# HGRN2 scan of a decoder step: sample outputs as rows on four groups of 32 TensorE columns, and scores of levels 32 and 64 on all column groups

## The chip, the cores and the metric

The kernel runs on one core of a Trainium2 chip. The metric is the device time of one execution in microseconds (us), as the median over the runs of a kernel.

## The reference

One inference step of a hybrid decoder layer: a SwiGLU half step, an input projection, an HGRN2 group of 4 heads (key and value size 128) beside a Mamba-2 group, an output projection, and a second SwiGLU half step. There are 1048 tokens: 16 meta tokens and 1024 prompt tokens, which are one sequence, and 8 samples of one token each, every one with a state of its own. Per HGRN2 head and sequence:

```
f = lb + (1-lb) sigmoid(u_f);  k = 1 - f;  v = u_i;  q = silu(u_q)
S_t = diag(f_t) S_{t-1} + k_t v_t^T          # 128x128
o_t = S_t^T q_t
```

For a sample that is one update of its state and one product of the updated state with its q. For the prompt the kernel computes the same by chunks of 128 tokens.

## The kernel before, in words

The phases follow one another: the first SwiGLU step, the input projection, the Mamba-2 scan, the four HGRN2 heads, the output projection, the second SwiGLU step. TensorE (PE) executes in the order in which the program is written. The order of the other engines (DVE, ACT, POOL, and SP, which issues the DMAs) is made by a scheduler, from dependencies and its own costs; an edit anywhere can so move instructions of theirs that it doesn't touch.

**Cover.** Between the steps of a head PE works off matmuls of the input projection that are still due, as `Fill` hands them out: `fill(n)` puts n steps of three matmuls (L163 to L165, some 350 columns each, 128x128 weights) into PE's order. While PE does these, DVE and ACT prepare the head's next step.

**One head** (`hgrn_scan`, L1713 to L1917). Its tensors lie with the 128 features on partitions and tokens along the free axis. First v is transposed; the columns of q, f and kg (k) that belong to the 8 samples are copied into a small tile qs, which has one buffer (L1740 to L1742). Then comes a tree of levels m = 1, 2, 4, ..., 64. A level computes scores within each chunk of 128 tokens, between the first and the second half of every block of 2m tokens, and then multiplies q of the second halves and k of the first by products of f (L1847 and L1848 on DVE). The next level's scores need these products, and L1847 and L1848 of a level need its scores to have been read. After each level stands a `fill` of 5 to 9 steps.

- Diagonal blocks (L1778) and levels below 32 (L1816): tiles of 32 stationary columns, round the four column groups of the array.
- Level 32 (L1807): for each of 8 chunks two matmuls of 32 stationary and 32 moving columns, which go to groups 0 and 2. ACT copies them into pp (L1810), two copies.
- Level 64: for each chunk one matmul of 64 stationary and 64 moving columns, always on the first 64 columns of the array; one copy.

**Samples of a head.** `load` (L1748) brings four states and, spread over the partitions, four rows v. `samples` (L1754) makes k v on ACT (L1758) and f S + k v on DVE (L1759). `outputs` (L1790) makes S^T q: it stands behind the scores of level 32 for samples 0 to 3 and behind those of level 64 for samples 4 to 7. For each sample the state, 128x128, is the stationary tile, and one column of q moves (L1792); the four results are columns of one PSUM tile, which ACT copies into os8 (L1793).

**After the tree.** kg is transposed in eight 128x128 pieces (L1873) and one of 16 columns (L1876), ACT copies these to kt and kt8 (L1874, L1877), `fill(4)`, state products of each chunk (L1887), a chain of DVE steps over the chunk states (L1892, L1895), `fill(6)`, and the chunks' outputs (L1906, L1908). os8 is first read after the scan, where the head's output is normalised (L1926, L1931).

**Mamba samples.** The updates of the 8 Mamba samples' states are independent of the heads: loads (L1538, L1539), a scaling on ACT (L1543), an update on DVE (L1544), a reduction on DVE (L1551), a store (L1552). The scheduler puts most of them into the time of head 0.

Tiles of 128x512 for state data come from a ring of 8 buffers (names r), 256-column tiles from a ring of 9 (names t), PSUM tiles for all of this from a ring of 4 (names mis).

Of the kernel before, what the change touches and what calls it, by code (L numbers as in the profile page):

```python
# [12 lines left out]
AF = mybir.ActivationFunctionType  # L13
ALU = mybir.AluOpType
# [3 lines left out]
P = 128  # L18
# [4 lines left out]
TP = NM + SEQ  # L23
NS = 8
T = TP + NS
# [1687 lines left out]
def hgrn_scan(K, a, o, hd, u, fill):  # L1713

    nc = K.nc
    q, f, kg, v = u["q"], u["f"], u["k"], u["v"]
# [3 lines left out]
    def small(tag, r, w=P):  # L1720
        return K.sml.tile([r, w], F32, tag=tag, name=K.uid(tag), bufs=1)
# [5 lines left out]
    for half in range(2):  # L1727
        ps = K.psm()
# [4 lines left out]
    ps = K.psm()  # L1733
# [3 lines left out]
    nc.scalar.copy(vs8, ps[:8, P : 2 * P])  # L1737
    vd = K.dram.tile([8, P], F32, name=K.uid("vd"))
    nc.sync.dma_start(vd, vs8)
    qs = small("qs", P, 24)  # L1740
    for i, src in enumerate((q, f, kg)):
        nc.scalar.copy(qs[:, 8 * i : 8 * i + 8], src[:, TP:T])  # L1742


    states = {}

    def load(b0):
        sb = K.raw().rearrange("p (b v) -> p b v", b=4)  # L1748
        vb = K.raw().rearrange("p (b v) -> p b v", b=4)
        nc.sync.dma_start(sb, a["state_hgrn"][0, b0 : b0 + 4, hd].rearrange("b k v -> k b v"))  # L1750
        nc.sync.dma_start(vb, vd[b0 : b0 + 4].partition_broadcast(P))
        states[b0] = sb, vb

    def samples(b0):  # L1754
        sb, vb = states[b0]
        for i in range(4):
            b = b0 + i
            nc.scalar.activation(vb[:, i], vb[:, i], AF.Identity, scale=qs[:, 16 + b : 17 + b])  # L1758
            nc.vector.scalar_tensor_tensor(sb[:, i], sb[:, i], qs[:, 8 + b : 9 + b], vb[:, i], ALU.mult, ALU.add)  # L1759
        nc.sync.dma_start(o["hgrn_sample"][0, b0 : b0 + 4, hd].rearrange("b k v -> k b v"), sb)  # L1760
        states[b0] = sb

# [7 lines left out]
    pv = pp.rearrange("p (c t) -> p c t", c=8)  # L1770
# [3 lines left out]
    ps = K.psm()  # L1774
# [11 lines left out]
    load(0)  # L1786
    os8 = small("os8", P, NS)

    def outputs(b0):
        ps = K.psm()  # L1790
        for i in range(4):
            nc.tensor.matmul(ps[:, i : i + 1], states[b0][:, i], qs[:, b0 + i : b0 + i + 1], start=True, stop=True)  # L1792
        nc.scalar.copy(os8[:, b0 : b0 + 4], ps[:, 0:4])  # L1793

    copies, copies8 = [diagonal], [small_diagonal]
    fe = f
    for li, m in enumerate(LEVELS):
        nb = 64 // m
        w = TP if m < 16 else 1024
        ps = K.psm()  # L1800
        qv = qf[:, :1024].rearrange("p (c b s i) -> p c b s i", c=8, s=2, i=m)
        if m >= 32:

            for c in range(8):
                for b in range(nb):
                    r = slice(2 * m * b, 2 * m * b + m)
                    nc.tensor.matmul(ps[r, m * c : m * c + m], kg[:, P * c + 2 * m * b : P * c + 2 * m * b + m], qv[:, c, b, 1], start=True, stop=True)  # L1807
            for b in range(nb):
                r = slice(2 * m * b, 2 * m * b + m)
                nc.scalar.copy(pv[r, :, 2 * m * b + m : 2 * m * b + 2 * m], ps[r, : 8 * m].rearrange("p (c i) -> p c i", c=8))  # L1810
        else:
            nb = 16 // m
            for c in range(8):
                for j in range(4):
                    r = slice(32 * j, 32 * j + 32)
                    nc.tensor.matmul(ps[r, 16 * c : 16 * c + 16], kg[:, P * c + 32 * j : P * c + 32 * j + 32], qv[:, c, nb * j : nb * j + nb, 1], start=True, stop=True)  # L1816

            def copy(m=m, nb=nb, ps=ps):
                pvm = pd.rearrange("p c (b s i) -> p c b s i", s=2, i=m)[:, :, :, 1]
                nc.vector.copy_predicated(pvm, K.mask[m].rearrange("p (b i) -> p b i", i=m)[:, None].broadcast_to([P, 8, nb, m]), ps[:, :P].rearrange("p (c b i) -> p c b i", c=8, i=m))  # L1820
                if m == 16:
                    for r in range(0, P, 32):
                        nc.scalar.copy(pv[r : r + 32, :, r : r + 32], pd[r : r + 32])

            copies.append(copy)
        if li == 0:
            s8 = K.psm()
            nc.tensor.matmul(s8[:16, 64:80], kg[:, 1024:TP], q[:, 1024:TP], start=True, stop=True)
        if m < 16:
            q8 = qf[:, 1024:TP].rearrange("p (b s i) -> p b s i", s=2, i=m)  # L1830
            nc.tensor.matmul(s8[:16, 8 * li : 8 * li + 8], kg[:, 1024:TP], q8[:, :, 1], start=True, stop=True)

            def copy8(li=li, m=m):
                nc.vector.copy_predicated(p8.rearrange("p (b s i) -> p b s i", s=2, i=m)[:, :, 1], K.mask[m][:16, 0:8].rearrange("p (b i) -> p b i", i=m), s8[:16, 8 * li : 8 * li + 8].rearrange("p (b i) -> p b i", i=m))

            copies8.append(copy8)
        if m >= 32:
            outputs({32: 0, 64: 4}[m])
        n = w // (2 * m)
        fv = fe[:, : w // m].rearrange("p (b s) -> p b s", s=2)  # L1840
        qw = qf[:, :w].rearrange("p (b s i) -> p b s i", s=2, i=m)
        kw = kg[:, :w].rearrange("p (b s i) -> p b s i", s=2, i=m)
        mid = 512 // (2 * m)
        with K.tc.high_priority(1000):
            for bs in (slice(0, mid), slice(mid, n)):
                k = bs.stop - bs.start
                nc.vector.tensor_mul(qw[:, bs, 1], qw[:, bs, 1], fv[:, bs, 0:1].broadcast_to([P, k, m]))  # L1847
                nc.vector.tensor_mul(kw[:, bs, 0], kw[:, bs, 0], fv[:, bs, 1:2].broadcast_to([P, k, m]))  # L1848
        fn = fp.tile([P, n])
        nc.vector.tensor_mul(fn, fv[:, :, 0], fv[:, :, 1])  # L1850
        if m == 8:
            f16 = fn
        fe = fn
        for copy in copies:
            copy()
        copies = []
        if m == 8:
            for copy in copies8:
                copy()
        if m == 4:  # L1860
            load(4)
        if m in (2, 16):
            samples({2: 0, 16: 4}[m])
        fill((9, 9, 8, 8, 7, 7, 7)[li] if hd < 3 else 7 if li < 2 else 5)
# [4 lines left out]
    for half in range(2):  # L1869
        ps = K.psm()  # L1870
# [4 lines left out]
    ps = K.psm()  # L1875
    nc.tensor.transpose(ps[:16, 0:P], kg[:, 1024:TP], K.ident)  # L1876
    nc.scalar.copy(kt8, ps[:16, 0:P])  # L1877
    fill(4)
    ss = K.slot("s", w=1024).rearrange("p (c v) -> p c v", c=8)
    s9 = small("s9", P, P)  # L1880
    for part in range(3):
        pu = K.psm()
        cc = range(4 * part, min(4 * part + 4, NC))
        for c in cc:
            i = c - 4 * part
            lk, lv = (kt[:, P * c : P * c + P], vt[:, P * c : P * c + P]) if c < 8 else (kt8, vt8)
            nc.tensor.matmul(pu[:, i * P : (i + 1) * P], lk, lv, start=True, stop=True)  # L1887
        for c in cc:
            i = c - 4 * part
# [11 lines left out]
    for half in range(2):  # L1901
        po = K.psm()
        for i in range(4):
            c = 4 * half + i
# [4 lines left out]
        c0 = NM if half == 0 else 0  # L1909
# [172 lines left out]
def body(ctx, tc, a, o):  # L2082
# [172 lines left out]
    with K.tc.manual_schedule(engines={mybir.EngineType.PE}):  # L2255
# [8 lines left out]
        for hd in range(NH):  # L2264
            fill.until(f"v{hd}")
            fill(4)
            if hd == 3:
                fill.jobs, fill.period = [lambda i=i: opa.update({i: split_opa(i)}) for i in (0, 2, 1, 3)], 13
            pieces = hgrn_scan(K, a, o, hd, us[hd], fill)
            g = us[hd]["g"] if hd < 3 else None  # L2270
            if hd == 0:
                fill.jobs, fill.period = jobs, 4
            if hd < 3:
                fill.until(f"g{hd}")
                hgrn_out(K, hd, pieces, g, "s", fill)
            if hd == 2:
                fill.until("z0")
                fill(10)
                ssm_norm(K, 0, "s", fill)
            if hd < 2:  # L2280
                spill(hd, g)
            elif hd == 2:
                kept.append(g)
# [160 lines left out]
```

## Time and profile before

| what | us |
|---|---|
| runs of before | 1937.75, 1937.73, 1942.81 |
| median | 1937.75 |
| span of the profiled execution | 1938.2 |
| PE busy in it | 1911.5 (99%) |
| DVE busy | 1533.1 (79%) |
| ACT busy | 845.8 (44%) |
| POOL busy | 96.8 (5%) |

The profile is of one further execution; the page gives its span and no other time for it. Its rows name engine, line, operation, the tile written and the tiles read, and sizes as partitions times elements; "x4" is a count of instructions. A bracket such as [1.57 <-DVE u L1848] is idle time of the engine just before the row, and what ended it. Ends of matmuls are modelled, so starts are what to subtract.

### The profile page before, as it was taken

How to read it: one execution, taken by the hardware profiler on the slowest of the kernel's cores; microseconds unless marked ns; L12 is line 12 of the kernel's file. 1: busy time of each engine (PE TensorE's matmuls, PEld its weight loads, DVE VectorE, ACT ScalarE, POOL GpSimd, SP SyncE). 2: the span in 40 equal slices, each digit the busy share in tenths (PEclk: the TensorE clock that was granted, in tenths of full speed). 3: DMA queues.
4: the chain of work that ended last, by engine and by line, in shares of the span. 5: the costliest groups of instructions: out<-in, count | busy, mean ns of one | idle time of the engine just before them, and what ended most of it. 6: DMA issues, size and time to landing. Idle time of an engine off the chain costs nothing.

```text
span 1938.2 us, 41058 instructions
## 1 busy us (share of the span) xinstructions
PE 1911.5 (99%) x16571; PEld 1882.1 (97%) x16571; DVE 1533.1 (79%) x2802; ACT 845.8 (44%) x1639; POOL 96.8 (5%) x155
## 2 busy tenths in 40 slices
PE   7999999999999999999999999999999999999998
PEld 7999999999999999999999989999999999999997
DVE  8888888888788777575766567998888888878965
ACT  8432322323534644475553455742232333354353
POOL 5000000000000410000000002200000000000000
PEclk9999999999999999999999999999999999999999
DMA  7232333325977542221544154233333333587862
GB/s 229 78 116 83 101 104 94 110 90 170 302 233 234 165 150 57 61 93 40 156 133 109 42 168 148 70 109 102 93 100 96 108 99 110 162 249 228 281 184 78
DMA packets 324071, 258.48 MB, mean 133 GB/s; under 512 B 17761, under 2 KB 299617, under 8 KB 323873
## 3 DMA queue, kind: packets, MB, share of 16 engines
q1 hardware_dynamic: 323640, 255.80, 43.5%
q8 instruction: 131, 2.15, 0.5%
q14 instruction: 60, 0.48, 0.1%
q0 software_dynamic: 224, 0.04, 0.0%
q10 hardware_dynamic: 16, 0.00, 0.0%
HBM read 191.84 MB, written 64.01 MB: 132 GB/s over the span
## 4 chain that ended last, share of the span: by engine, by line
PE 92%; DVE 4%; ACT 2%; issue 1%; DMA 1%; DVEq 0%; POOL 0%; ACTq 0%; POOLq 0%
PE acc L163 27%; PE acc L165 27%; PE acc L164 27%; PE mis L163 2%; PE mis L164 2%; PE mis L165 2%; PE mis L1816 1%; PE mis L1464 0%; PE mis L1887 0%; PE mis L1460 0%; ACT u L348 0%; PE mis L1792 0%; DVE t L303 0%; PE mis L1455 0%; PE mis L1906 0%
## 5 line engine op out<-in xcount | busy, mean ns | idle before, releaser
L163 PE MATMUL acc<-u,ws 128*128 128x258 f32 (+4 forms) x4226 | 1235.7, 293 | 0.7 <-DVE u L1095 0.3
L164 PE MATMUL acc<-u,ws 128*128 128x258 f32 (+4 forms) x4226 | 1225.2, 290 | 2.4 <-DVE u L354 2.2
L165 PE MATMUL acc<-u,ws 128*128 128x258 f32 (+4 forms) x4226 | 1225.7, 290 | 1.4 <-DVE ws L468 1.3
L164 PEld LDWEIGHTS acc<-u,ws 128*128 128x128 f32 x4226 | 802.1, 190 | 5.3 <-DVE u L354 2.8
L163 PEld LDWEIGHTS acc<-u,ws 128*128 128x128 f32 x4226 | 799.7, 189 | 4.2 <-issue 1.0
L165 PEld LDWEIGHTS acc<-u,ws 128*128 128x128 f32 x4226 | 798.9, 189 | 2.3 <-DVE ws L468 1.9
L468 DVE TENSOR_TENSOR ws<-r,ws 128x512 fp32r<-128x512 f32 x276 | 190.2, 690 | 73.5 <-ACT ws L464 73.3
L464 ACT CAST ws<-r 128x512 fp32r<-128x512 f32 x276 | 160.2, 616 | 15.3 <-ACT ws L464 8.6
L460 DVE TENSOR_TENSOR r<-r,r 128x512 f32<-128x512 f32 x176 | 121.5, 691 | 1.7 <-DMA r<-in_w_ffn_up_dram 0.2
L683 ACT ACTIVATE t<-t 128x516 f32<-128x516 f32 (+1 forms) x41 | 26.2, 639 | 211.1 <-DVE t L671 211.1
L714 ACT ACTIVATE t<-t 128x524 f32<-128x524 f32 (+1 forms) x47 | 30.0, 639 | 196.8 <-DVE t L671 196.8
L850 DVE TENSOR_TENSOR u<-u,u 128x1048 fp32r<-128x1048 f32 (+3 forms) x84 | 97.0, 1156 | 5.5 <-ACT u L846 5.1
L232 POOL TENSOR_TENSOR t<-t,t 128x262 f32<-128x262 f32 (+1 forms) x56 | 56.8, 1024 | 800.6 <-ACT t L231 690.9
L671 DVE TENSOR_TENSOR t<-t,u 128x524 f32<-128x524 f32 (+1 forms) x135 | 93.0, 696 | 2.9
L158 DVE TENSOR_TENSOR ws<-r,ws 128x512 fp32r<-128x512 f32 x88 | 60.8, 702 | 35.8 <-ACT ws L157 35.6
L907 ACT CAST ws<-u 128x512 fp32r<-128x512 f32 (+1 forms) x72 | 42.1, 585 | 102.6 <-DVE u L902 102.6
L846 ACT CAST u<-u 128x1048 fp32r<-128x1048 f32 (+3 forms) x84 | 82.8, 988 | 0.0
L907 ACT CAST ws<-r 128x512 fp32r<-128x512 f32 (+1 forms) x84 | 48.0, 582 | 70.9 <-DVE r L902 32.1
L936 DVE SCALAR_TENSOR_TENSOR s<-acc,s 128x524 f32<-128x524 f32 (+3 forms) x86 | 53.8, 648 | 31.5 <-PE acc L165 31.3
L912 DVE TENSOR_TENSOR ws<-r,ws 128x512 fp32r<-128x512 f32 (+1 forms) x84 | 56.3, 680 | 22.8 <-ACT ws L907 22.8
L157 ACT CAST ws<-r 128x512 fp32r<-128x512 f32 x88 | 54.0, 618 | 36.5 <-PE acc L165 31.0
L912 DVE TENSOR_TENSOR ws<-u,ws 128x512 fp32r<-128x512 f32 (+1 forms) x72 | 47.4, 658 | 26.5 <-ACT ws L907 26.5
(444 smaller groups left out, 2324.7 us busy)
## 6 DMA issues: line engine op xcount, KB each, us to landing
r<-in_w_ffn_down_dram SPq DMA_DIRECT2D x128, 256.0 KB
hd<-s SPq DMA_DIRECT2D x93, 258.0 KB
r<-in_w_ffn_gate_dram SPq DMA_DIRECT2D x88, 256.0 KB
r<-in_w_ffn_up_dram SPq DMA_DIRECT2D x88, 256.0 KB
hd<-s SPq DMA_DIRECT2D x77, 262.0 KB
u<-hd SPq DMA_DIRECT2D x36, 516.0 KB
u<-hd SPq DMA_DIRECT2D x28, 524.0 KB
r<-in_w_in_dram SPq DMA_DIRECT2D x56, 256.0 KB
```

What stands on the lines that cost most here:

```text
L158: self.nc.vector.tensor_sub(lo, src, hi.bitcast(F32))
L163: mm(ps, whi, xhi, start=first, stop=False, skip_group_check=more)
L164: mm(ps, whi, xlo, start=False, stop=False, skip_group_check=more)
L165: mm(ps, wlo, xhi, start=False, stop=last, skip_group_check=more)
L460: self.K.nc.vector.tensor_tensor(self.raw[p], self.raw[x], self.raw[y], op)
L464: self.K.nc.scalar.copy(self.w[p][:, : self.n * P], self.raw[p])
L468: self.K.nc.vector.tensor_sub(t[:, 512 : 512 + w], self.raw[p], t[:, :w].bitcast(F32))
L671: nc.vector.tensor_mul(t, t if src is None else src, spread.lanes(i, cs))
L846: K.nc.scalar.copy(hi, lo.bitcast(F32))
L850: K.nc.vector.tensor_sub(lo, lo.bitcast(F32), hi.bitcast(F32))
L907: nc.scalar.copy(w[p, j, g][:, : n * P], src)
L912: nc.vector.tensor_sub(t[:, 512 : 512 + n * P], box[0], t[:, : n * P].bitcast(F32))
```

## The change

qs grows from 24 to 48 columns: q in columns 0 to 7, zeros in 8 to 31 (a POOL memset), f in 32 to 39, k in 40 to 47. `outputs` swaps the operands: the stationary tile is now the 32 columns of q and zeros, the state moves, 128 columns of it, and the four samples go to the four column groups, so that each gives 32 rows of which one is wanted. ACT copies 128x128 into a new tile `rows` (256 columns, from the ring t). A new step `columns` turns both halves with two 128x128 transposes, and two ACT copies pick every 33rd column into os8; it stands behind the transposes of kg, ahead of `fill(4)`. The scores of levels 32 and 64 of odd chunks go to the column groups that were idle (1 and 3; columns 64 to 127), and the copies out of PSUM become twice as many of half the size.

```diff
-    qs = small("qs", P, 24)
-    for i, src in enumerate((q, f, kg)):
-        nc.scalar.copy(qs[:, 8 * i : 8 * i + 8], src[:, TP:T])
+    qs = small("qs", P, 48)
+    nc.gpsimd.memset(qs[:, NS:32], 0.0)
+    for c0, src in ((0, q), (32, f), (40, kg)):
+        nc.scalar.copy(qs[:, c0 : c0 + NS], src[:, TP:T])
...
+    rows = K.t(2 * P)
+
     def outputs(b0):
+        ps = K.psm()[:, :P]
+        for i in range(4):
+            nc.tensor.matmul(ps[32 * i : 32 * i + 32], qs[:, :32], states[b0][:, i], start=True, stop=True)
+        nc.scalar.copy(rows[:, 32 * b0 : 32 * b0 + P], ps)
+
+    def columns():
         ps = K.psm()
-        for i in range(4):
-            nc.tensor.matmul(ps[:, i : i + 1], states[b0][:, i], qs[:, b0 + i : b0 + i + 1], start=True, stop=True)
-        nc.scalar.copy(os8[:, b0 : b0 + 4], ps[:, 0:4])
+        for b0 in (0, 4):
+            nc.tensor.transpose(ps[:, 32 * b0 : 32 * b0 + P], rows[:, 32 * b0 : 32 * b0 + P], K.ident)
+            nc.scalar.copy(os8[:, b0 : b0 + 4], ps[:, 33 * b0 : 33 * b0 + 100 : 33])
...
             for c in range(8):
                 for b in range(nb):
+                    r0 = 2 * m * b + c % 2 * m
+                    nc.tensor.matmul(ps[r0 : r0 + m, c // 2 * m : c // 2 * m + m], kg[:, P * c + 2 * m * b : P * c + 2 * m * b + m], qv[:, c, b, 1], start=True, stop=True)
+            for b in range(nb):
+                for e in range(2):
                     r = slice(2 * m * b, 2 * m * b + m)
-                    nc.tensor.matmul(ps[r, m * c : m * c + m], kg[:, P * c + 2 * m * b : P * c + 2 * m * b + m], qv[:, c, b, 1], start=True, stop=True)
-            for b in range(nb):
-                r = slice(2 * m * b, 2 * m * b + m)
-                nc.scalar.copy(pv[r, :, 2 * m * b + m : 2 * m * b + 2 * m], ps[r, : 8 * m].rearrange("p (c i) -> p c i", c=8))
+                    r0 = 2 * m * b + e * m
+                    nc.scalar.copy(pv[r, e::2, 2 * m * b + m : 2 * m * b + 2 * m], ps[r0 : r0 + m, : 4 * m].rearrange("p (c i) -> p c i", c=4))
...
     ps = K.psm()
     nc.tensor.transpose(ps[:16, 0:P], kg[:, 1024:TP], K.ident)
     nc.scalar.copy(kt8, ps[:16, 0:P])
+    columns()
     fill(4)
```

Three places of the order show what it does to the engines. Sizes in these rows are those of the stationary or written tile and the moving columns. Behind L1760 the changed file's line numbers are higher by up to 13: L1807 becomes L1816, L1792 L1795, L1847 and L1848 become L1858 and L1859, L1820 L1831, L1874 L1885, L1810 L1821, L1793 L1796.

PE in head 0 at level 32, before: the scores (L1807), the outputs of samples 0 to 3 (L1792), and the cover.

```order
L165 MATMUL acc_11353<-u_8458,ws_11115 128x344
L1807 MATMUL mis_11363<-s_10876,u_10026 32x32 x16
L1792 MATMUL mis_11382<-qs_10900,r_10963 128x1 x4
L163 MATMUL acc_11353<-u_8459,ws_11115 128x344
L164 MATMUL acc_11353<-u_8467,ws_11115 128x344
```

The same place now, and the transposes of kg with what follows.

```order
L165 MATMUL acc_11355<-u_8458,ws_11117 128x344
L1816 MATMUL mis_11365<-s_10876,u_10026 32x32 x16
L1795 MATMUL mis_11386<-r_10964,qs_10900 32x128 x4
L163 MATMUL acc_11355<-u_8459,ws_11117 128x344
...
L1884 MATMUL mis_11467<-ident,u_10026 128x128 x4
L1884 MATMUL mis_11473<-ident,u_10026 128x128 x4
L1887 MATMUL mis_11479<-ident,u_10026 16x128
L1801 MATMUL mis_11482<-ident,t_10969 128x128 x2
```

Nothing moved on PE: four matmuls have other operands, two transposes are new.

DVE in head 0 before, between the copy of level 4's scores (L1820) and the scaling of level 8 (L1847, L1848); r_11583 and r_11612 are states of Mamba samples.

```order
L1820 COPY_PREDICATED t_10928<-mask_8815,mis_11136 128x32x4
L1544 SCALAR_TENSOR_TENSOR r_11583<-r_11583,s_8852,t_11587 128x128
L1544 SCALAR_TENSOR_TENSOR r_11583<-r_11583,s_8852,t_11590 128x128
...
L1551 ISA t_11628,s_8852<-r_11583,r_11584 128x128
L1551 ISA s_8852 128x1
L1847 TENSOR_TENSOR s_10876<-s_10876,s_11008 128x32x8
L1848 TENSOR_TENSOR u_10026<-u_10026,s_11008 128x32x8
L1847 TENSOR_TENSOR s_10876<-s_10876,s_11008 128x33x8
```

DVE at the same place now, and further on between the scaling of level 32 (8x32) and that of level 64 (4x64).

```order
L1831 COPY_PREDICATED t_10929<-mask_8815,mis_11138 128x32x4
L1858 TENSOR_TENSOR s_10876<-s_10876,s_11010 128x32x8
L1859 TENSOR_TENSOR u_10026<-u_10026,s_11010 128x32x8
L1858 TENSOR_TENSOR s_10876<-s_10876,s_11010 128x33x8
...
L1859 TENSOR_TENSOR u_10026<-u_10026,s_11010 128x8x32
L1544 SCALAR_TENSOR_TENSOR r_11593<-r_11593,s_8852,t_11597 128x128
L1544 SCALAR_TENSOR_TENSOR r_11593<-r_11593,s_8852,t_11600 128x128
...
L1858 TENSOR_TENSOR s_10876<-s_10876,s_11010 128x4x64
```

Before, eight updates (L1544) and three reductions (L1551, two rows each) stood at the first place, and three more updates and a reduction ahead of level 32's scaling; now there is none at either, seven updates stand at the second place, and the rest comes later.

ACT in head 0 now, from the copies of level 32's scores (L1821) to those of the transposed kg (L1885); L1543 is the Mamba samples' scaling.

```order
L1821 COPY s_10925<-mis_11365 32x4x32 x4
L1796 COPY t_10969<-mis_11386 128x128
L1543 ACTIVATE t_11597<-r_11594,s_8852 128x128
L1543 ACTIVATE t_11600<-r_11594,s_8852 128x128
...
L1543 ACTIVATE t_11696<-r_11693,s_8852 128x128
L1543 ACTIVATE t_11699<-r_11693,s_8852 128x128
L1543 ACTIVATE t_11702<-r_11693,s_8852 128x128
L1885 COPY s_11465<-mis_11467 128x512
L1885 COPY s_11465<-mis_11473 128x512
```

Before, the first L1543 of the samples stood ahead of level 8; now it stands behind L1796. Three of the fourth group of samples (r_11693) stand just ahead of the copies of kg. On SP the loads of the third and fourth group (L1538, L1539) now stand ahead of the stores (L1552), and the last of them waits until PE has read the second group of states in `outputs`, whose buffer it takes over.

More of the change, by code (lines that the diff above doesn't have):

```diff
@@ L1757, in samples @@
             b = b0 + i
-            nc.scalar.activation(vb[:, i], vb[:, i], AF.Identity, scale=qs[:, 16 + b : 17 + b])
-            nc.vector.scalar_tensor_tensor(sb[:, i], sb[:, i], qs[:, 8 + b : 9 + b], vb[:, i], ALU.mult, ALU.add)
+            nc.scalar.activation(vb[:, i], vb[:, i], AF.Identity, scale=qs[:, 40 + b : 41 + b])
+            nc.vector.scalar_tensor_tensor(sb[:, i], sb[:, i], qs[:, 32 + b : 33 + b], vb[:, i], ALU.mult, ALU.add)
         nc.sync.dma_start(o["hgrn_sample"][0, b0 : b0 + 4, hd].rearrange("b k v -> k b v"), sb)
```

## The prediction

> **What bounds the kernel now.** I read the chain of waits first, as it says which engine sets the end.
>
> ```profile
> PE 92%; DVE 4%; ACT 2%; issue 1%; DMA 1%; DVEq 0%; POOL 0%; ACTq 0%; POOLq 0%
> PE acc L163 27%; PE acc L165 27%; PE acc L164 27%; PE mis L163 2%; PE mis L164 2%; PE mis L165 2%; PE mis L1816 1%; PE mis L1464 0%; PE mis L1887 0%; PE mis L1460 0%; ACT u L348 0%; PE mis L1792 0%; DVE t L303 0%; PE mis L1455 0%; PE mis L1906 0%
> ```
>
> TensorE (PE) holds 92% of the chain. A microsecond taken out of PE's row of work comes off the end, unless PE then waits for it; work on DVE and ACT counts only where PE waits for them. So I went to the PE timeline of head 0 at levels 32 and 64 (columns: start, length from first start to last modelled end, engine, line, tiles). Lengths of pipelined matmuls overlap, so I subtract starts.
>
> ```profile
> 942.61 0.70 PE L1807 MATMUL mis<-s,u 128*32 128x32 f32 x32
> 943.24 1.05 PE L1792 MATMUL mis<-qs,r 128*128 128x1 f32 x8
> 944.15 0.40 PE L163 MATMUL acc<-u,ws 128*128 128x344 f32 x1
> 944.40 0.32 PE L164 MATMUL acc<-u,ws 128*128 128x344 f32 x1
> 944.55 0.32 PE L165 MATMUL acc<-u,ws 128*128 128x344 f32 x1
> 947.65 1.15 PE L1807 MATMUL mis<-s,u 128*64 128x64 f32 x16
> 948.72 1.05 PE L1792 MATMUL mis<-qs,r 128*128 128x1 f32 x8
> 949.64 0.41 PE L163 MATMUL acc<-u,ws 128*128 128x344 f32 x1
> ```
>
> Level 32 takes 944.15 - 942.61 = 1.54: scores 0.63, sample outputs 0.91. Level 64 takes 949.64 - 947.65 = 1.99: scores 1.07, outputs 0.92. The program has 4 matmuls where the trace has 8: each is run as two passes. An outputs pass streams one column, yet costs 0.11.
>
> **Part by part: PE's own work.** The grouping by line gives all four heads (min, mean, max ns of one), and these are the nearest rows for tiles spread over column groups and for moving tiles of 128 columns.
>
> ```profile
> L1792 PE MATMUL mis<-qs,r x64: 250/250/272, 943.2 to 1138.5; 128*128 128x1 f32 x64
> L1778 PE MATMUL mis<-u,u x256: 196/196/217, 914.5 to 1111.0; 128*32 128x32 f32 x128
> 914.54 0.73 PE L1778 MATMUL mis<-u,u 128*32 128x32 f32 x62
> 833.84 1.09 PE L1460 MATMUL mis<-s,s 128*64 128x128 f32 x16
> 834.86 1.13 PE L1464 MATMUL mis<-s,s 128*128 128x256 f32 x4
> 953.05 1.03 PE L1873 MATMUL mis<-ident,u 128*128 128x128 f32 x8
> 953.92 0.27 PE L1876 MATMUL mis<-ident,u 128*16 128x128 f32 x1
> ```
>
> Three prices come from them. 32-column tiles going round four groups, moving 32 columns (L1778): (0.73 - 0.196)/61 = 8.7 ns a start. A pass that moves 128 columns, alone on the array (L1873): (953.92 - 953.05)/8 = 0.109. L1460 sends 16 such passes to two groups in 834.86 - 833.84 = 1.02; if the two groups run side by side that is 8 rounds of 0.109 = 0.87 and 0.15 left for the change to a tile of another width, which I take as the price of a change.
>
> Scores of level 32 go from two groups to four: 32 x 0.0087 = 0.28 for 0.63. They stood before a change of width, and now the outputs have 32 columns too, so none stands here. Outputs: 8 passes over four groups are two rounds, 2 x 0.109 + 0.15 for the change to the projection's tiles = 0.37 for 0.91. Level 32: 0.65 for 1.54, -0.89. Bounds of the outputs: 0.22 (no change to pay) and 8 x 0.109 + 0.15 = 1.02 (no overlap at all). I take two rounds, since L1460 moves the same 128 columns on column groups, and L1778's 8.7 ns on four of them is far under one pass.
>
> Scores of level 64: 1.07 is 0.92 for 16 starts on one group and a change of 0.15. On two groups 0.46 + 0.15 (64 to 32 columns) = 0.61; outputs 0.37 again. 0.98 for 1.99, -1.01.
>
> columns(): two transposes as in L1873, +0.22 (bound 0.44, were each two passes). A head: -0.89 - 1.01 + 0.22 = -1.68. The 64 passes of the grouped row are four equal heads: **-6.7**.
>
> **A stall in head 0.** The same timeline further up, the windows around it (columns: us, busy us and instructions of PE, PEld, DVE, ACT, POOL, then PE clock, DMA share, GB/s), and DVE's and ACT's rows.
>
> ```profile
> 934.71 0.32 PE L165 MATMUL acc<-u,ws 128*128 128x348 f32 x1
> 936.60 0.45 PE L1816 MATMUL mis<-s,u 128*32 128x16 f32 x32 [1.57 <-DVE u L1848]
> 937.19 0.45 PE L1816 MATMUL mis<-s,u 128*32 128x16 f32 x32 [0.15 <-DVE u L1848]
> 938.47 0.49 PE L165 MATMUL acc<-u,ws 128*128 128x348 f32 x1
> 941.65 0.41 PE L164 MATMUL acc<-u,ws 128*128 128x344 f32 x1
> 934.70:936.60 1.90, 0.33 (x4) 0.07 (x3) 1.90 (x11) 0.98 (x3) 0.00 (x0) 1.00 0.53 148
> 938.40:941.80 3.40, 3.40 (x14) 3.40 (x13) 2.02 (x6) 0.06 (x1) 0.00 (x0) 0.50 0.55 170
> 932.26 1.23 DVE L1544 SCALAR_TENSOR_TENSOR r<-r,s,t 128x128 f32<-128x128 f32 x4 [1.96 <-ACT t L1543]
> 935.70 0.42 DVE L1847 TENSOR_TENSOR s<-s,s 128x256 f32<-128x256 f32 x1
> 936.71 0.42 DVE L1848 TENSOR_TENSOR u<-u,s 128x264 f32<-128x264 f32 x1
> ```
>
> PE waits 1.57 + 0.15 for the scaling of level 8, which stands late on DVE behind the Mamba samples (L1544, L1551). Then 3.4 us run at a clock of 0.50: eleven starts between 938.47 and 941.65 at 0.29 each, where 944.40 to 944.55 shows 0.15, so 11 x 0.14 = 1.5 lost. The changed program's DVE order has none of these sample instructions ahead of level 8's scaling: it follows the copy of level 4 directly. Both wait and half clock should go: 1.57 + 0.15 + 1.5 = **-3.2**. What is late next in head 0 is under the rivals.
>
> On the clock, the Trainium skill ("TensorE: Matmul & The Clock Gate", "Why this matters for your kernels") says that PE gaps of over about 3 us bring half clock. The trace shows it right after a wait of 1.57, so the rule's gap isn't needed here; by the rule the half clock would have another cause and stay, and the saving would be 1.7 instead of 3.2.
>
> **What should be hidden.** Rows for ACT's copies, DVE's slack in head 1, and the Mamba samples on ACT.
>
> ```profile
> L1810 ACT COPY s<-mis x12: 347/364/580, 945.6 to 1137.8; 32x256 f32<-32x256 f32 x8, 64x512 f32<-64x512 f32 x4
> L1793 ACT COPY os<-mis x8: 162/162/163, 946.4 to 1138.8; 128x4 f32<-128x4 f32 x8
> 1005.56 0.41 DVE L1848 TENSOR_TENSOR u<-u,s 128x256 f32<-128x256 f32 x1
> 1007.42 0.80 PE L1807 MATMUL mis<-s,u 128*64 128x64 f32 x10
> 931.83 1.28 ACT L1543 ACTIVATE t<-r,s 128x128 f32<-128x128 f32 x4 [4.80 <-DMA r<-sbd]
> 941.74 1.02 ACT L1543 ACTIVATE t<-r,s 128x128 f32<-128x128 f32 x3 [6.07 <-DMA r<-sbd]
> 949.87 0.99 ACT L1543 ACTIVATE t<-r,s 128x128 f32<-128x128 f32 x3
> 954.10 1.06 ACT L1874 COPY s<-mis 128x512 f32<-128x512 f32 x2
> 938.12 0.46 SPq L1539 DMA_DIRECT2D r<-sbd  x1
> 955.93 1.95 PE L1887 MATMUL mis<-s,s 128*128 128x128 f32 x16
> ```
>
> Copies out of PSUM: level 32 has four of half size, level 64 two, the rows' copy is 128x128 rather than 128x4, and columns() has two copies of 128x4. At 0.16 to 0.35 each that is about 1.1 more ACT a head. Nothing on PE reads them before the transposes of columns() or the outputs after fill(6), so I cost it at nothing; were a transpose to wait for its rows, PE would lose up to one copy, 0.35. The POOL memset of 24 columns is one small instruction a head; if it is late, the copies into qs wait, with the samples' updates behind, and they have levels 1 to 16 to spare: nothing. Earlier PE work leaves less slack to DVE: tightest is level 64 of head 1, where DVE ends at 1005.56 + 0.41 = 1005.97 and PE comes at 1007.42, 1.45; level 32 gives back 0.89 ahead of it, so some 0.56 stays. In head 0, too, DVE has no sample instruction left ahead of level 32's scaling, on which level 64 waits. Were that cover gone, PE would wait for what is short.
>
> **Sum.** The rows are of an execution with a span of 1938.2, 0.45 above the median of 1937.75. -6.7 - 3.2 = -9.9, put on the median: 1937.75 - 9.9 = **1927.9**.
>
> **Rivals.**
>
> 1. Half clock stays though the wait goes.
>
> ```profile
> 985.00:1000.00 15.00, 15.00 (x275) 14.25 (x275) 13.35 (x60) 7.88 (x23) 0.24 (x3) 1.00 0.78 226
> ```
>
> For it: in the window 934.70:936.60 the clock is still 1.00, and the half follows only at 938.4, behind the small tiles of level 8, so these rather than the wait may bring it. Against: this window of head 1 holds levels 4 to 16 without a wait, at 1.00. 1927.9 + 1.5 = 1929.4. Chance 0.10.
>
> 2. Column groups take turns when they move 128 columns: outputs 1.02 instead of 0.37, eight times +0.65 = +5.2, 1933.1. For it: no row before has four groups at this length. Against: L1460's pairs and L1778. Chance 0.07. The Trainium skill's same page ("Part 3: Packing small matmuls", what overlaps) says that a weight load overlaps matmuls in flight only if it is for other rows of the array; all tiles here use all rows, so by it this rival would hold. L1778's 8.7 ns a start, with a load for each, speaks against it.
>
> 3. Slower: the Mamba samples keep their pace and only start later. Before, ACT began them at 931.83 and the third of the fourth group ended at 949.87 + 0.99 = 950.86, 19.0 later. In the changed ACT order the first stands behind level 32's copies, at about 941.5 (level 32 on PE at 939.4, being 3.2 earlier, scores and outputs 0.65, copies some 1.5), and these three stand ahead of the two kt copies, which L1887 needs: 941.5 + 19.0 + 1.06 = 961.6. PE would be there at about 951 (955.93 less 3.2 and 1.68). A wait of 10.6, half clock again 1.5: 1927.9 + 12.1 = 1940.0. It outweighs the gain from a wait of 9.9 - 1.5 = 8.4. For it: the order. Against: the 19 were waits for DMA (the 4.80 and 6.07 above), and the loads are now issued ahead of the stores, some of them long before. Chance 0.08, half of it far enough for slower.
>
> 4. The same place, short. The last load goes out when PE has read the second group of states, about 944.3; 938.12 to 941.74 shows 3.6 for such a load, then 0.99 and 1.06: 950.0 against PE's 951. If a load is slower by 2.7, a wait of 1.7 and half clock return: 1927.9 + 3.2 = 1931.1. Chance 0.11, 0.04 of it within the bound below.
>
> 5. A second stall goes too:
>
> ```profile
> 1117.65 0.21 PE L1816 MATMUL mis<-s,u 128*32 128x16 f32 x2 [1.69 <-issue]
> 1119.00:1124.00 5.00, 5.00 (x85) 4.66 (x84) 3.96 (x9) 2.63 (x6) 0.00 (x0) 0.66 0.73 240
> ```
>
> In head 3 PE loses 1.69 to something that the profile doesn't show, then 5 x 0.34 = 1.7 to the clock. PE reaches it some 8 earlier; if its cause is tied to a fixed moment it may vanish: 1927.9 - 3.4 = 1924.5. Nothing in the change removes it. Chance 0.08.
>
> **How the numbers follow.** The forecast itself has 0.56, and alone the range 1926 to 1930 (outputs at 0.22 gain 1.2; two groups at a time, 0.59, cost 1.8). The range 1924.0 to 1933.2 takes in rivals 1, 2, 4 and 5 and leaves out 3 and what I haven't thought of. A difference of 0.3%, 5.8 us, can be told from none: faster is under 1931.9, slower over 1943.6. Faster: 0.56 + 0.10 + 0.07 + 0.08 = 0.81; within: rival 2, parts of 3 and 4, 0.15; slower: the rest of 3, 0.04.
>
> **What would show it.** In the PE timeline of every head: level 32 about 0.65 from first score to the next L163, level 64 about 0.98, the step of columns() 0.22. In head 0: no wait at level 8 and a clock of 1.00 after it; no wait ahead of the state products (L1887 before). It is wrong if outputs take about 1.0 (rival 2), if a wait of some microseconds for ACT stands between the kt transposes and the state products of head 0 (3, 4), or if the four heads save less than 5 us together.

## The result: 1934.22 us against 1939.78, and the profile after

| kernel | median, us | runs | span of the profiled execution |
|---|---|---|---|
| before | 1939.78 (1936.20 to 1942.81) | 12 | 1938.2 |
| changed | 1934.22 (1931.09 to 1937.94) | 12 | 1932.9 |

The ratio is 0.9973, with a 95% interval of 0.9966 to 0.998: 5.2 us less, where 9.9 less had been forecast. The time lies above the range (1924.0 to 1933.2). Part of that distance is the yardstick: the three runs shown had a median of 1937.75 for before, the twelve have 1939.78. In what follows the differences count, not the times.

PE's row of work at levels 32 and 64 of head 0 came out as worked out. The same timeline as in the prediction, in the changed kernel:

```profile
936.26 0.32 PE L165 MATMUL acc<-u,ws 128*128 128x348 f32 x1
936.51 0.74 PE L1827 MATMUL mis<-s,u 128*32 128x16 f32 x64
940.71 0.46 PE L1816 MATMUL mis<-s,u 128*32 128x32 f32 x32
940.99 0.45 PE L1795 MATMUL mis<-r,qs 128*32 128x128 f32 x8
941.36 0.43 PE L163 MATMUL acc<-u,ws 128*128 128x344 f32 x1
...
944.88 0.69 PE L1816 MATMUL mis<-s,u 128*64 128x64 f32 x16
945.49 0.43 PE L1795 MATMUL mis<-r,qs 128*32 128x128 f32 x8
945.85 0.42 PE L163 MATMUL acc<-u,ws 128*128 128x344 f32 x1
```

Level 32 takes 941.36 - 940.71 = 0.65 (was 1.54), level 64 takes 945.85 - 944.88 = 0.97 (was 1.99). Level 8 (936.51) follows its cover without a wait. What went wrong stands a little further down, PE first, then ACT at the same time:

```profile
949.25 1.04 PE L1884 MATMUL mis<-ident,u 128*128 128x128 f32 x8
950.12 0.27 PE L1887 MATMUL mis<-ident,u 128*16 128x128 f32 x1
950.23 0.27 PE L1801 MATMUL mis<-ident,t 128*128 128x128 f32 x1
951.73 0.33 PE L1801 MATMUL mis<-ident,t 128*128 128x128 f32 x1 [1.22 <-ACT os L1802]
951.81 0.40 PE L163 MATMUL acc<-u,ws 128*128 128x344 f32 x1
```

```profile
949.55 0.98 ACT L1543 ACTIVATE t<-r,s 128x128 f32<-128x128 f32 x3
950.43 1.05 ACT L1885 COPY s<-mis 128x512 f32<-128x512 f32 x2
951.37 0.25 ACT L1888 COPY kt<-mis 16x128 f32<-16x128 f32 x1
951.53 0.15 ACT L1802 COPY os<-mis 128x4 f32<-128x4 f32 x1
951.58 0.40 ACT L1543 ACTIVATE t<-r,s 128x128 f32<-128x128 f32 x1
952.10 0.16 ACT L1802 COPY os<-mis 128x4 f32<-128x4 f32 x1
```

The two transposes of `columns` start 1.50 apart, and the bracket says for whom the second waits: for ACT's copy of the first into os8 (L1802). That copy takes 0.15, but stands in ACT's queue behind two copies of kt and the one of kt8, and in head 0 also behind three scalings of Mamba samples. PE stands still until 951.53 + 0.15. From the first kt transpose to the cover it is 951.81 - 949.25 = 2.56 here, where it was 0.90. The other heads show the same without the three scalings; head 1:

```profile
1008.84 1.03 PE L1884 MATMUL mis<-ident,u 128*128 128x128 f32 x8
1009.82 0.27 PE L1801 MATMUL mis<-ident,t 128*128 128x128 f32 x1
1010.79 0.33 PE L1801 MATMUL mis<-ident,t 128*128 128x128 f32 x1 [0.70 <-ACT os L1802]
1010.87 0.41 PE L163 MATMUL acc<-u,ws 128*128 128x344 f32 x1
```

Cover matmuls of the projection are the same in both kernels. I laid them side by side in the two traces, number by number, and took down where the distance between them grows or shrinks (changed less before, us):

| place | difference |
|---|---|
| all that comes before the heads | +1.6 |
| the stall at level 8 of head 0 and its half clock | -3.4 |
| levels 32 and 64, four heads | 4 x (-0.89 - 1.02) = -7.6 |
| kt transposes and columns(), four heads | 1.67 + 1.14 + 1.18 + 1.14 = +5.1 |
| idle time of PE that the profile calls issue, heads 2 and 3, with the half clock behind it in head 3 of before | +1.0 and -1.9 |
| sum | -5.2 |

Only the third and the fourth row, -2.5 together, are PE's own work and waits under the change in all four heads. The first row stands ahead of all that was edited: it is +3.1 up to 897, less some 1.5 because before's clock was 0.50 from 897.46 to 900.88, with no wait of PE ahead of it.

### The profile page after: what moved, and what is told of

Same layout as the page of the kernel before. It is cut to its first block, busy times and chain, and to the rows that moved or that the text cites. A ratio compares the mean times of both kernels' runs of the same rounds, so it can differ in the third digit from the quotient of the medians.

```text
span 1932.9 us, 41114 instructions
## 1 busy us (share of the span) xinstructions
PE 1903.4 (98%) x16579; PEld 1870.8 (97%) x16579; DVE 1533.3 (79%) x2802; ACT 849.3 (44%) x1659; POOL 90.0 (5%) x159
## 4 chain that ended last, share of the span: by engine, by line
PE 86%; DVE 7%; ACT 2%; DMA 1%; issue 1%; SPq 0%; DVEq 0%; POOL 0%; ACTq 0%; POOLq 0%
PE acc L163 25%; PE acc L165 25%; PE acc L164 25%; PE mis L163 2%; PE mis L165 2%; PE mis L164 2%; DMA r<-in_w_ffn_down_dram 1%; DVE u L850 1%; DVE s L936 1%; DVE u L902 1%; DVE ws L912 1%; PE mis L1827 1%; PE mis L1464 0%; ACT ws L907 0%; PE mis L1899 0%
```

## The experiments

Each ratio is to runs of before that were taken together with the experiment (their medians were 1939.81, 1939.05 or 1938.02), with its 95% interval; "less" is worked out from it.

The theory after the first look: **the second transpose writes the PSUM tile that ACT is still reading for the first copy, so PE waits for a copy that is queued behind the copies of kt; this takes back 4.2 us.** The rivals: PE would wait for ACT at that place or the next one anyway; the scores or the outputs bring less than their rows say; the stall in head 0 is not the change's to remove.

**1. Copies behind both transposes.**

```diff
         for b0 in (0, 4):
             nc.tensor.transpose(ps[:, 32 * b0 : 32 * b0 + P], rows[:, 32 * b0 : 32 * b0 + P], K.ident)
+        for b0 in (0, 4):
             nc.scalar.copy(os8[:, b0 : b0 + 4], ps[:, 33 * b0 : 33 * b0 + 100 : 33])
```

> The changed kernel with columns() in another order: both transposes first, then the two copies into os8. In the changed kernel the step from the first kt transpose to the cover takes 2.57 in head 0 and 2.04 to 2.08 in the others, 0.90 before. Theory A: the second transpose, into the PSUM tile that ACT is still reading for the first, waits for that copy, and the copy stands on ACT behind those of kt and kt8. Then the wait goes: the step takes 0.90 + 0.22 = 1.12 in every head, 1.45 + 3 x 0.94 = 4.3 less, about 1930.0 where the changed kernel has 1934.2; against before a ratio of 0.995. Rival B: PE only waits elsewhere, since ACT's queue is no shorter: the state products after fill(4) wait for the same kt copies, by about 1 in each head, and the time stays at 1933 to 1934, 0.997.

Measured: 1931.97, ratio 0.9955 (0.9942 to 0.9967). PE in head 0:

```profile
950.27 1.04 PE L1885 MATMUL mis<-ident,u 128*128 128x128 f32 x8
951.14 0.27 PE L1888 MATMUL mis<-ident,u 128*16 128x128 f32 x1
951.25 0.38 PE L1801 MATMUL mis<-ident,t 128*128 128x128 f32 x2
951.39 0.40 PE L163 MATMUL acc<-u,ws 128*128 128x344 f32 x1
```

951.39 - 950.27 = 1.12, and 1.12 in the other three heads. There is no wait ahead of the state products in any head, so rival B falls. Theory A holds, for the step to the digit. The time is 8.7 less than before (6.4 to 11.3), where the changed kernel had 5.2; the two were not run together, and the intervals touch, so it is the step that carries this.

**2. A PSUM tile for each transpose.**

```diff
-        ps = K.psm()
         for b0 in (0, 4):
-            nc.tensor.transpose(ps[:, 32 * b0 : 32 * b0 + P], rows[:, 32 * b0 : 32 * b0 + P], K.ident)
-            nc.scalar.copy(os8[:, b0 : b0 + 4], ps[:, 33 * b0 : 33 * b0 + 100 : 33])
+            ps = K.psm()
+            nc.tensor.transpose(ps[:, :P], rows[:, 32 * b0 : 32 * b0 + P], K.ident)
+            nc.scalar.copy(os8[:, b0 : b0 + 4], ps[:, b0 : b0 + 100 : 33])
```

> The changed kernel with a PSUM tile for each of the two transposes of columns(), each followed by its copy as in the change. Theory A (the second transpose waits because it writes the PSUM tile that the first copy reads): that wait goes; but the ring has four PSUM tiles, and the fifth (two for kt, one for kt8, two here) takes over that of the first half of kt, whose copy must have been made: by the rows of the changed kernel 950.98 in head 0 and 1010.02 in head 1, so the step from the first kt transpose to the cover takes about 1.9 in head 0 and 1.3 in the others, where it was 2.57 and 2.04, and 1.12 with the copies behind both transposes. 2.8 less than the changed kernel in all, 1931.4, ratio 0.996. Rival: what PE waits for is ACT's turn, whichever tile is written: the steps stay at 2.57 and 2.04, 1934.2, 0.9973.

Measured: 1932.58, ratio 0.9968 (0.9956 to 0.9981); steps of 1.91, 1.36, 1.41 and 1.36. Head 0:

```profile
949.91 1.03 PE L1884 MATMUL mis<-ident,u 128*128 128x128 f32 x8
950.90 0.27 PE L1801 MATMUL mis<-ident,t 128*128 128x128 f32 x1
951.74 0.33 PE L1801 MATMUL mis<-ident,t 128*128 128x128 f32 x1 [0.57 <-ACT s L1885]
951.82 0.41 PE L163 MATMUL acc<-u,ws 128*128 128x344 f32 x1
```

Now the bracket names L1885: the second transpose no longer waits for the copy into os8, but for the buffer of the first half of kt, which the ring of four hands it. The two transposes write different columns of one tile in the changed kernel, and the first copy reads no column that the second transpose writes. Yet it waited, and with a tile of its own this wait is gone: the order goes by tile, not by column. Whether it has to, no run here asks.

**3. columns() behind the cover.**

```diff
-    columns()
     fill(4)
+    columns()
```

> The changed kernel with columns() behind fill(4) instead of ahead of it. Theory A: by then ACT has made the copies of kt and kt8, so the second transpose waits only for its own copy to be made, some 0.5 in heads 1 to 3 and 0.3 more in head 0, where a scaling of the Mamba samples stands ahead of it on ACT. Against the changed kernel's waits of 1.45 and 3 x 0.94 that is 2.0 to 2.5 less, about 1932, ratio 0.996. Rival: the place is of no account, since the copy comes behind other work on ACT anyway; 1934, 0.9973.

Measured: 1932.18, ratio 0.9964 (0.9951 to 0.9977). Head 1, PE and then ACT:

```profile
1011.68 0.27 PE L1801 MATMUL mis<-ident,t 128*128 128x128 f32 x1
1012.21 0.33 PE L1801 MATMUL mis<-ident,t 128*128 128x128 f32 x1 [0.25 <-ACT os L1802]
1011.99 0.16 ACT L1802 COPY os<-mis 128x4 f32<-128x4 f32 x1 [1.33 <-PE mis L1801]
```

The starts are 0.53 apart instead of 0.97. ACT had been idle for 1.33, so the copy starts 0.31 behind the first transpose; it takes 0.16, and the second transpose follows 0.06 later. In head 0 it is the same 0.53; the scaling that I had put ahead of the copy there was done in time. So the same dependency costs more or less with the queue in front of the copy.

**4. The scores alone, and 5. the rows alone.** The first is before with one hunk of the change alone, the new placing of the scores of levels 32 and 64 with their copies; the second is the changed kernel with this hunk taken back.

```diff
             for c in range(8):
                 for b in range(nb):
+                    r0 = 2 * m * b + c % 2 * m
+                    nc.tensor.matmul(ps[r0 : r0 + m, c // 2 * m : c // 2 * m + m], kg[:, P * c + 2 * m * b : P * c + 2 * m * b + m], qv[:, c, b, 1], start=True, stop=True)
+            for b in range(nb):
+                for e in range(2):
...
-                    nc.tensor.matmul(ps[r, m * c : m * c + m], kg[:, P * c + 2 * m * b : P * c + 2 * m * b + m], qv[:, c, b, 1], start=True, stop=True)
```

> Before with the scores of levels 32 and 64 on all column groups alone; outputs and os8 as before. Theory A: PE saves 0.63 - 0.28 less one change of width that is still to be paid (0.15), so 0.20 at level 32, and 0.46 at level 64: 0.66 a head, 2.6 in all. In DVE's order of head 0 the Mamba samples stand ahead of level 8 as before, so the stall of 1.57 and the half clock behind it stay. 1939.8 - 2.6 = 1937.2, ratio 0.9987. Rival: the stall goes with any change of PE's pace in the heads: 3.2 more, 1934.0, 0.9970.

Measured: 1935.95, ratio 0.9981 (0.9973 to 0.999), 3.7 less; the interval reaches from 1.9 to 5.2. Level 32 (938.90 to 940.20) takes 1.30 and level 64 1.53, 0.70 a head less than before. But the stall was neither kept nor lost as expected: with DVE's order as in before, PE waited at level 8 only a little.

```profile
934.03 0.32 PE L165 MATMUL acc<-u,ws 128*128 128x348 f32 x1
934.42 1.04 PE L1818 MATMUL mis<-s,u 128*32 128x16 f32 x64
...
938.90 0.46 PE L1807 MATMUL mis<-s,u 128*32 128x32 f32 x32
939.29 1.05 PE L1792 MATMUL mis<-qs,r 128*128 128x1 f32 x8
940.20 0.40 PE L163 MATMUL acc<-u,ws 128*128 128x344 f32 x1
```

Scores begin 934.42 - 934.03 = 0.39 behind the cover's last start (0.25 without a wait, as at 936.26 and 936.51 above). My order-based reason for the stall was at least not the whole of it, and experiments 7 to 9 go after that. Ahead of the state products of head 0, PE now waited 0.90 for a copy of kt (L1876), so getting there earlier was not all gain.

> The changed kernel with the scores of levels 32 and 64 as before; outputs as rows and columns() as changed. Theory A: outputs 0.54 to 0.56 less at each of the two levels, 4.4 in all; the step of columns() 1.15 to 1.65 longer than before, 5.1 in all; DVE's order of head 0 is that of the changed kernel, so the stall goes, 3.2. 1939.8 - 4.4 + 5.1 - 3.2 = 1937.3, ratio 0.9987. Rival: the rows hold no stall's worth, as half clock comes from the small tiles: the wait goes, the half clock stays, 1938.8, 0.9995.

Measured: 1937.86, ratio 0.9987 (0.9978 to 0.9996), 2.5 less, as by theory A; the interval also holds its rival. The waits of columns() are there, 1.54 in head 0:

```profile
954.38 0.33 PE L1801 MATMUL mis<-ident,t 128*128 128x128 f32 x1 [1.54 <-ACT os L1802]
```

So the rows without the scores, as changed, are worth little: their gain at the levels (4.4) goes back at columns() (5.1), and by theory A the 2.5 is what the stall gave.

**6. Outputs on one column group**, with columns() as in experiment 10.

```diff
-        ps = K.psm()[:, :P]
+        ps = K.psm()
         for i in range(4):
-            nc.tensor.matmul(ps[32 * i : 32 * i + 32], qs[:, :32], states[b0][:, i], start=True, stop=True)
-        nc.scalar.copy(rows[:, 32 * b0 : 32 * b0 + P], ps)
+            nc.tensor.matmul(ps[:32, P * i : P * i + P], qs[:, :32], states[b0][:, i], start=True, stop=True)
+        for i in range(4):
+            nc.scalar.copy(rows[32 * i : 32 * i + 32, 32 * b0 : 32 * b0 + P], ps[:32, P * i : P * i + P])
```

> The changed kernel with columns() as both transposes and then one copy of all eight columns into os8, and with the four matmuls of each outputs() on one group of 32 columns, side by side in its PSUM tile (ACT then copies four pieces of 32x128). It prices the column groups. Theory A: eight passes of 0.109 one behind the other and the change of width 0.15 make 1.02 where four groups take 0.37; level 32 takes about 1.30, level 64 about 1.62, 5.2 in all over the same with four groups (1931 to 1932): 1936.7, ratio 0.9985. Rival: column groups take turns anyway when they move 128 columns, and the 0.37 comes from shorter passes; then both steps stay at 0.65 and 0.97, and 1932, 0.996.

Measured: 1935.67, ratio 0.9984 (0.9974 to 0.9995); the same with four groups is experiment 10.

```profile
939.52 1.04 PE L1795 MATMUL mis<-r,qs 128*32 128x128 f32 x8
940.49 0.43 PE L163 MATMUL acc<-u,ws 128*128 128x344 f32 x1
```

The outputs take 940.49 - 939.52 = 0.97 on one group, and took 941.36 - 940.99 = 0.37 on four. Column groups do work side by side at 128 moving columns, though all four tiles use all rows. The Trainium skill ("TensorE: Matmul & The Clock Gate", "Part 3: Packing small matmuls") says that a weight load overlaps matmuls in flight only for other rows of the array, though the same section also lets a load into the background weight buffer go ahead. The rows speak against the former as it stands; to which buffer a load goes, they don't show. The loads of L1795 take 109 ns each in the trace of the changed kernel, eight of them are 0.87, and the whole step is 0.37:

```profile
L1795 PEld LDWEIGHTS mis<-r,qs x64: 106/109/113, 941.0 to 1131.9; 128*32 128x32 f32 x64
```

**7. Samples held back, everything else as before.** `issue_after` adds one edge: ACT's scaling of the Mamba samples may stand only behind its copy of the first sample outputs of head 0.

```diff
-        nc.scalar.copy(os8[:, b0 : b0 + 4], ps[:, 0:4])
+        done = nc.scalar.copy(os8[:, b0 : b0 + 4], ps[:, 0:4])
+        if hd == 0 and b0 == 0:
+            K.hold = done
...
-            nc.scalar.activation(up, rows[:, j // 2], AF.Identity, scale=dx[:, j, b : b + 1])
+            with K.tc.issue_after(K.hold.ins):
+                nc.scalar.activation(up, rows[:, j // 2], AF.Identity, scale=dx[:, j, b : b + 1])
```

> Before with one edge more: ACT's scaling of the Mamba samples stands behind the copy of the first sample outputs of head 0. PE's instructions are those of before; DVE's and ACT's order of the samples in head 0 becomes that of the changed kernel. Theory A: the stall ahead of level 8 and the half clock behind it go, and nothing else: 3.2 less, 1936.6, ratio 0.9984. Rival: the samples, started later, keep PE waiting at the state products for the kt copies that stand behind them on ACT; a wait of some microseconds there eats the gain, ratio 1.000 or more.

Measured: 1936.91, ratio 0.9986 (0.9977 to 0.9995), 2.7 less (1.0 to 4.5). Level 8 in head 0, without a wait:

```profile
935.08 0.32 PE L165 MATMUL acc<-u,ws 128*128 128x348 f32 x1
935.33 0.74 PE L1819 MATMUL mis<-s,u 128*32 128x16 f32 x64
```

No wait has taken its place at the state products. So a good part of the change's gain has nothing to do with column groups: an edge on ACT, with PE's work untouched, brings it too (how much of the 5.2, the interval leaves open).

**8 and 9. Before, twice more.** Nothing is edited; the question is how firm the 3.2 was.

> Before, unchanged, for a second profile. Theory A: the wait ahead of level 8 of head 0 is a race, since DVE and ACT hold 14 and 8 instructions of the Mamba samples ahead of level 8's scaling, and these wait for the broadcast rows to land: in the first profile ACT's scaling began 17.3 behind the first diagonal score and PE waited 1.57; with the same order in scores_only it began 15.9 behind it and PE waited 0.15. So the wait lies somewhere between 0.1 and 2, with the half clock behind it only in some of the profiles. Rival: scores_only was spared because of its change; then before shows 1.5 to 1.6 and half clock again.

> Before, unchanged, for a third profile; the same as for the second: by theory A a wait ahead of level 8 that goes with the landing of the broadcast rows, by the rival 1.5 to 1.6 and half clock again.

Measured: 1935.29 and 1939.49, one execution each. ACT's first scaling and level 8 on PE in the second profile:

```profile
929.87 1.28 ACT L1543 ACTIVATE t<-r,s 128x128 f32<-128x128 f32 x4 [3.36 <-DMA r<-sbd]
934.67 0.32 PE L165 MATMUL acc<-u,ws 128*128 128x348 f32 x1
934.92 0.74 PE L1816 MATMUL mis<-s,u 128*32 128x16 f32 x64
```

and in the third:

```profile
932.84 1.28 ACT L1543 ACTIVATE t<-r,s 128x128 f32<-128x128 f32 x4 [4.57 <-DMA r<-sbd]
937.41 0.45 PE L1816 MATMUL mis<-s,u 128*32 128x16 f32 x32 [0.62 <-DVE u L1848]
```

The same program waits 1.57, not at all and 0.62 at level 8. It goes by the landing of the broadcast rows, for which ACT waits: in these three and scores_only, the longer it takes from the head's first score to ACT's first scaling, the longer PE waits: 15.4 (929.87 less 914.51) and no wait, 15.9 and 0.14 in scores_only, 16.6 (932.84 less 916.28) and 0.62, 17.3 and 1.57. Both later profiles have a smaller wait at level 64 of head 0 instead (0.39 and 0.55 for L1848), and none of half clock. Theory A: it is a race, and the rival falls.

**10. The version that the experiments point to**: as 1, with one copy, since the wanted columns lie 33 apart over both halves.

```diff
-            nc.scalar.copy(os8[:, b0 : b0 + 4], ps[:, 33 * b0 : 33 * b0 + 100 : 33])
+        nc.scalar.copy(os8, ps[:, 0:232:33])
```

> The version that the experiments point to: the changed kernel with columns() as both transposes and then a single copy that takes all eight columns, 33 apart, into os8. Theory A: PE does the same as with the copies behind both transposes, one ACT copy of 0.15 a head less, which hides: a step of 1.12 in every head and the same time, 1931 to 1932, ratio 0.995 to 0.996. Rival: the longer copy with 8 columns, or a wait at the state products, gives something back; 0.997.

Measured: 1930.11, ratio 0.9951 (0.9938 to 0.9965), steps of 1.12 in every head. That is 9.5 less than before (6.8 to 12.0). The interval lies just under that of the changed kernel (0.9966 to 0.998), which was not run beside it; from 1 it can't be told.

**11. Longer waits, for the clock.**

```diff
-            nc.scalar.copy(os8[:, b0 : b0 + 4], ps[:, 33 * b0 : 33 * b0 + 100 : 33])
+            for _ in range(1 if b0 else (1, 8, 16, 28)[hd]):
+                nc.scalar.copy(os8[:, b0 : b0 + 4], ps[:, 33 * b0 : 33 * b0 + 100 : 33])
```

> The changed kernel, in which the first copy into os8 is made 1, 8, 16 and 28 times in heads 0 to 3, so that PE waits longer ahead of the second transpose: about 1.2, 1.75, 3.0 and 4.75 of idle time. It asks what brings the half clock. Theory A: a wait of about 1.6 or more, as ahead of level 8 in the trace of before: a clock of 0.50 for some 3.4 us behind the waits of heads 1 to 3. Rival B, the rule of the Trainium skill (TensorE: Matmul & The Clock Gate, Why this matters for your kernels) that a gap must be over about 3 us: only in head 3, and perhaps head 2. Rival C, the small tiles of the levels bring it: none of the four, as only 128x128 tiles stand here. Time: 1934.2 and 0, 1.05, 2.25 and 4.05 of longer waits, 7.4, and 1.5 for each half clock.

Measured: 1943.7, one execution. The waits came out at 1.23, 2.06, 3.65 and 5.93. Heads 2 and 3, and four windows of 3.41 around them (the last three columns are PE clock, DMA share, GB/s):

```profile
1073.57 0.33 PE L1801 MATMUL mis<-ident,t 128*128 128x128 f32 x1 [3.65 <-ACT os L1803]
1144.90 0.47 PE L1801 MATMUL mis<-ident,t 128*128 128x128 f32 x1 [5.93 <-ACT os L1803]
```

```profile
1068.36:1071.78 3.42, 1.56 (x13) 1.28 (x12) 0.69 (x1) 3.19 (x13) 0.00 (x0) 1.00 0.00 0
1071.78:1075.19 3.41, 1.62 (x11) 1.62 (x12) 0.23 (x1) 2.67 (x12) 0.00 (x0) 1.00 0.00 0
1140.04:1143.46 3.42, 0.00 (x0) 0.00 (x0) 0.00 (x0) 2.89 (x18) 0.00 (x0) 1.00 0.42 135
1143.46:1146.87 3.41, 1.97 (x7) 1.97 (x8) 0.00 (x0) 2.63 (x11) 0.00 (x0) 0.50 0.00 0
```

Only the wait of 5.93 brought half clock, from 1143.46 on, while PE still waited; 2.06 and 3.65 left it at 1.00. Theory A of this experiment falls. Rival B holds for head 3, and allowed for either in head 2; rival C falls too, as large tiles alone stand around the wait of head 3.

## Why the prediction was wrong, point by point

- **Scores and outputs.** Right: 0.65 and 0.97 against 0.65 and 0.98 forecast, and one_group gives 0.97 for the outputs on one group, which I had put at 1.02. The three prices (a start, a pass of 128 columns, a change of width) carried over. Rival 2 is refuted.
- **columns(), the step that failed.** "Two transposes as in L1873, +0.22" counted PE's instructions and left out that a copy stands between them. I had costed the copies at nothing because "Nothing on PE reads them" before the outputs; but the second transpose writes the tile that the first copy reads, and waits for it. It cost 5.1 instead of 0.9. The price was there to be worked out: in the program the copies of kt and kt8 stand ahead of `columns`, ACT's order showed the two of kt behind three scalings, and L1874's row gave 1.06 for these two. copies_last, two_tiles and behind_cover each changed one thing about this wait, and the steps came within about 0.1 of what they should be by this cause, but for head 0 of behind_cover, which was 0.3 better. The place was even named as one that would show the prediction wrong (a wait for ACT "between the kt transposes and the state products"), but for rivals 3 and 4, by way of late samples; these did not come.
- **The stall in head 0.** Gone, as forecast, and by the step named: without the samples ahead of level 8's scaling, as in the changed kernel and in the eight experiments with its order of the samples, hold_samples among them, no profile has a wait there. One profile of hold_samples alone would not show it, since one of before has none either. But 3.2 was its price in one profile. In the two other profiles of before the same place and the next cost some 0.4, and some 1.2 (0.62 and 0.55). hold_samples puts its mean at 2.7, with an interval from 1.0 to 4.5.
- **Half clock** went with the wait. Rival 1 did not come. That a wait of this length brings it is not fixed, though; see the grid in the last section.
- **Rivals 3 and 4** did not come: the profile of the changed kernel has no wait ahead of the state products. Of their late samples only the three scalings ahead of the copies of kt are left, by which the step of head 0 is 0.5 longer than the others.
- **The sum.** -9.9 forecast; +4.2 for columns() and about +0.5 for the stall (3.2 less the 2.7 of hold_samples) give -5.2, which was measured. That it fits to the tenth is luck, as the stall's 2.7 could be 1.7 more or less. With the wait removed, copies_last has -8.7 and one_copy -9.5, and their intervals (6.4 to 11.3 and 6.8 to 12.0) hold the 9.9, so the rest of the sum stood.
- **The range and the chances.** Less the median of 1937.75, the range reached from -13.75 to -4.55, and -5.2 would lie in it; but it was made wide for rivals 1, 2, 4 and 5, none of which came. On a time under 1931.9 the prediction had put 0.81, on the band above it, in which 1934.22 lies, 0.15. And the span of 1938.2 was taken to lie 0.45 above the median, though a time is not a span: the changed kernel's profiled run has 1934.65 for a span of 1932.9.
- **Rival 5**, the issue stall of head 3, did not vanish: it was 1.37 in the changed kernel without half clock, 1.65 and 1.39 in the later profiles of before, 2.99 in copies_last. It differs from one profile to the next of the same kernel, so the -1.9 in the table above is not to be credited to the change.

## What to carry to other kernels

When a step is added to the path, follow its tiles and not only its instructions: here a matmul that writes a tile from which another engine has yet to copy waited for that copy and for all that stood ahead of it in that engine's queue; so put all writes to a PSUM tile ahead of the first read. A stall that hangs on a DMA's landing has no single price in one profile; look at a second execution before it goes into a sum. And a scheduler may give an edit a gain (here some 2.7, of 1.0 to 4.5) that a single edge elsewhere would have given without it.

## What the runs showed of the hardware that had not been expected

**Half clock doesn't follow the length of a wait alone, and it comes on a grid.** In the prediction's trace it followed a wait of 1.57. In rows_only and scores_only waits of 1.58 and 1.70 that the profile calls issue, among the small tiles of head 3, left the clock at 1.00, and one of 2.99 in copies_last brought 0.50. Among large tiles 3.65 was still harmless and 5.93 was not. The Trainium skill's gap of about 3 us ("TensorE: Matmul & The Clock Gate", "Why this matters for your kernels") has the 1.57 and the 3.65 against it.

What the traces add: in each of the 13 profiles all changes of the granted clock lie whole multiples of 3.41 apart. In before the first window had no wait of PE, and half clock followed; the other two are those behind the waits of 1.57 and 1.69 (PE's busy time stands behind the length of the window):

```profile
894.05:897.46 3.41, 3.41 (x33) 2.96 (x34) 2.32 (x8) 0.34 (x2) 0.95 (x1) 1.00 0.00 0
897.46:900.88 3.42, 3.42 (x14) 3.42 (x13) 0.64 (x1) 0.39 (x1) 0.00 (x0) 0.50 0.00 0
938.42:941.84 3.42, 3.42 (x14) 3.42 (x13) 2.00 (x6) 0.10 (x1) 0.00 (x0) 0.50 0.56 170
1119.33:1122.74 3.41, 3.41 (x14) 3.23 (x12) 3.03 (x7) 1.27 (x4) 0.00 (x0) 0.50 0.78 266
```

From 900.88 to 938.42 it is 11 such stretches, from 941.84 to 1119.33 it is 52. So the clock is granted by stretches whose beginning no wait sets. It also fits longer_waits: 3.65 fell into two of them, 1.86 idle (3.42 - 1.56) and 1.79 (3.41 - 1.62), and 5.93 emptied a whole one. Idle time within a stretch does not decide alone either: 1.65 in before_again left the clock at 1.00, 1.64 in two_tiles brought 0.50, and the stretch from 894.05 had none. For part of that stretch PE worked on tiles of 16 rows (L1460, L1464), so small tiles may count for less than large ones. How the work in a stretch is weighed stays open.

**PE's idle time called issue** shows up in head 3 in every profile, at changing places within the small score tiles and 1.24 to 2.99 long, while the DMA queues move some 320 to 360 GB/s. Its cause stays open; no run was aimed at it.
